# Two-layer encoder trunk on one core: MLP products with both activation parts in 512 moving columns, and the norm chains placed first

## The chip, the cores and the metric

The kernel runs on one core of one Trainium2 chip. The metric is the device time of one execution in microseconds. A core has TensorE (PE) for matrix products, VectorE (DVE), ScalarE (ACT) and GpSimd (POOL) for work on tiles in SBUF, and DMA queues, here nearly all issued by SyncE (SP). PE adds its products up in PSUM, and DVE or ACT fetches them from there.

## The reference

Two layers run over 256 tokens of 2048 channels, in float32. Each layer has a modulated RMSNorm, a mixer with three kinds of heads behind one input projection, an output projection, a second modulated RMSNorm and an MLP with a squared ReLU and 8192 hidden channels. The six modulation vectors of a layer come from one condition vector and a matrix of 2048 x 12288.

```python
cond = jax.nn.silu(c)
for layer in range(DEPTH):                                   # 2
    mod = (cond @ ada_w[layer] + ada_b[layer])[:, None, :]
    sh_a, sc_a, g_a, sh_m, sc_m, g_m = jnp.split(mod, N_MOD, axis=-1)
    h = rmsnorm(x, norm_mix_w[layer]) * (1.0 + sc_a) + sh_a
    x = x + g_a * hybrid_mixer(h, ..., w_in[layer], ..., w_out[layer])
    h = rmsnorm(x, norm_mlp_w[layer]) * (1.0 + sc_m) + sh_m
    x = x + g_m * (jnp.square(jax.nn.relu(h @ w_ff1[layer])) @ w_ff2[layer])
return rmsnorm(x, final_norm_w)
```

## The kernel before

**Products.** Activations lie with channels on the partitions and the 256 tokens beside each other. Every large product is made of two parts per operand: ACT casts a weight tile to `wh` (L221), and DVE or POOL subtracts that from the tile and gives the rest, `wl` (L227; `pool_share` says what part goes to POOL). The activations have a high and a low part too (`hh`, `hl` for the normalised input). `mm_b` (L252 to L254) then does three matmuls of 256 columns for each 128x128 weight tile, with `wh` and the low part, `wl` and the high part, `wh` and the high part, into one of four quarters of a PSUM tile of 1024 columns (`pair`, named pj in the profile, of which there are two in turn). `mm_a` (L263 to L265) is the form of the mixer with 512 columns of weights moving.

**Stages.** Layer 0 has its input projection in groups of contraction tiles, with the modulation vectors coming in beside it; then the mixer heads, the output projection (four blocks `nb` of 512 columns, `residual` at L796 adds each to X), and the MLP. Weights come as chunks of 512 KB (`raw`, six buffers), 508 of them for the MLP. `ff1` makes a block of 512 hidden channels, `square` applies Relu (L964), Square (L969), a cast (L971) and a subtraction (L972) and so gives the block's two parts, `ff2` takes eight contraction tiles of two such blocks through four blocks of 512 output columns and adds them to X with four updates (L796) for each PSUM tile. `ff2_tail` does the last quarter of the last layer in narrower pieces.

**Norm chains.** Behind the last residual of a stage the sum of squares must be ready before the next stage can run. `stat_piece` squares a quarter of X and adds (L372 to L375), `stat_sum` adds over the partitions on PE (L383), a Newton iteration gives the inverse root (L393, L351 to L357), `stat_spread` sends it to all partitions (L401, then R by ACT at L405), and `h_make` forms the normalised input (L492 to L500). To keep PE at work meanwhile, `lead` computes the first block of the next projection from X that is not normalised yet (operand made at L432 to L437, products of 258 columns at L471 to L473) and `lead_out` corrects it afterwards (L485).

**Modulation vectors.** A tile of `ada_w` (512 KB, 380 of them) is multiplied by the condition on DVE (L283), with a running sum. `rate`, `step` and `pump` hand out how many of these tiles are issued in which stage; a DMA for them is issued behind the weight DMA nine back (WIN = 8).

**Order.** The Tile framework sets each engine's instruction order from the program order, priorities and simulated readiness; each engine then works through its list in that order. An instruction whose input is late holds up everything behind it on its engine.

## Time and profile before

| | us |
|---|---|
| median of 3 runs | 2548.88 |
| lowest and highest | 2541.46, 2551.96 |
| the profiled execution | 2549.75 |
| its span in the trace | 2548.0 |
| PE, DVE, ACT, POOL busy | 2450.1, 1583.2, 1180.9, 758.9 |

The mean granted clock of PE is 0.977 of 2.4 GHz. A row of a timeline begins with start and duration in us. The duration of a matmul contains its way through the array, and consecutive ones overlap, so what a matmul costs in a row is read from one start to the next. In groups by line, "x" is the count, and behind the bar stand busy us, mean ns of one, and idle us ahead with what ended it.

### The profile page before, as it was taken

Reading aid. Unit: us, or ns where it says so; the run is one execution under the profiler, and the core shown is the slowest. Engines: PE = TensorE matmul, PEld = TensorE weight load, DVE = VectorE, ACT = ScalarE, POOL = GpSimd, SP = SyncE. Lnnn points to the kernel's source line nnn. Section 1 sums busy time; section 2 is a strip of 40 time slices with the busy share of each in tenths; the row PEclk is TensorE's granted clock in tenths of the full one; section 3 lists DMA queues with packets and bytes.
Section 4 is the critical chain, followed back from the end, with each engine's and each line's share of the span. In section 5 each row is a group of like instructions: output and inputs, shape, how many; then the busy total and the mean of one; then the engine's idle time right before and its main releaser. Section 6 shows DMA issues by size and latency. Waiting matters only on the chain.

```text
span 2548.0 us, 46455 instructions
## 1 busy us (share of the span) xinstructions
PE 2450.1 (96%) x19016; PEld 2378.3 (93%) x19016; DVE 1583.2 (62%) x2427; ACT 1180.9 (46%) x1442; POOL 758.9 (30%) x314
## 2 busy tenths in 40 slices
PE   7999998979999999999989999999999999999997
PEld 6899977979999999999988989899999999999997
DVE  5867878788655444444478777656754555555554
ACT  4444455535544444444446446454644444344443
POOL 4786531212676766767650000000000000000000
PEclk8999999989999999999989999999999999999998
DMA  9899867788998888888867777555555555555552
GB/s 359 299 327 329 305 217 265 285 299 338 322 334 310 279 288 297 287 280 298 285 213 241 272 247 266 192 166 178 178 182 186 188 182 183 187 185 183 186 187 91
DMA packets 177246, 630.45 MB, mean 247 GB/s; under 512 B 19588, under 2 KB 24326, under 8 KB 177032
## 3 DMA queue, kind: packets, MB, share of 16 engines
q1 hardware_dynamic: 176600, 627.08, 70.8%
q8 instruction: 149, 2.44, 0.4%
q14 instruction: 65, 0.53, 0.1%
q10 hardware_dynamic: 432, 0.39, 0.1%
HBM read 625.30 MB, written 2.10 MB: 246 GB/s over the span
## 4 chain that ended last, share of the span: by engine, by line
PE 79%; DVE 9%; DMA 4%; issue 3%; POOL 3%; ACT 2%; SPq 0%; DVEq 0%; POOLq 0%; ACTq 0%
PE pj L253 23%; PE pj L252 23%; PE pj L254 23%; DMA ada<-ada_w 3%; POOL wl L227 3%; DVE ada L283 2%; PE pj L264 2%; PE pj L265 2%; PE pj L263 2%; DVE wl L227 2%; PE mx L620 1%; ACT wh L221 1%; DVE cv L709 1%; DVE blk L437 0%; DMA raw<-ada_w 0%
## 5 line engine op out<-in xcount | busy, mean ns | idle before, releaser
L221 ACT CAST wh<-raw 128x1024 fp32r<-128x1024 f32 x804 | 840.4, 1047 | 1129.8 <-PE pj L254 881.3
L227 POOL TENSOR_TENSOR wl<-raw,wh 128x1024 fp32r<-128x1024 f32 (+1 forms) x309 | 756.3, 2451 | 583.4 <-ACT wh L221 565.3
L227 DVE TENSOR_TENSOR wl<-raw,wh 128x1024 fp32r<-128x1024 f32 x495 | 615.7, 1246 | 487.4 <-ACT wh L221 486.7
L252 PE MATMUL pj<-hl,wh 128*128 128x256 f32 x2912 | 830.9, 286 | 9.5 <-DVE hl L500 8.2
L253 PE MATMUL pj<-hh,wl 128*128 128x256 f32 x2912 | 830.4, 285 | 7.2 <-DVE wl L227 7.2
L254 PE MATMUL pj<-hh,wh 128*128 128x256 f32 x2912 | 828.1, 284 | 0.0
L253 PE MATMUL pj<-blk,wl 128*128 128x256 f32 x2528 | 713.6, 282 | 6.6 <-DVE wl L227 5.2
L252 PE MATMUL pj<-blk,wh 128*128 128x256 f32 x2528 | 712.8, 282 | 2.8 <-ACT blk L538 1.5
L254 PE MATMUL pj<-blk,wh 128*128 128x256 f32 x2528 | 711.3, 281 | 0.0
L283 DVE SCALAR_TENSOR_TENSOR ada<-ada,cond 128x1024 f32<-128x1024 f32 x380 | 456.7, 1214 | 227.7 <-DMA ada<-ada_w 225.6
L252 PEld LDWEIGHTS pj<-hl,wh 128*128 128x128 f32 x2912 | 561.8, 193 | 10.7 <-DVE hl L500 8.9
L253 PEld LDWEIGHTS pj<-hh,wl 128*128 128x128 f32 x2912 | 562.4, 193 | 9.3 <-DVE wl L227 8.7
L254 PEld LDWEIGHTS pj<-hh,wh 128*128 128x128 f32 x2912 | 562.1, 193 | 0.2
L253 PEld LDWEIGHTS pj<-blk,wl 128*128 128x128 f32 x2528 | 478.5, 189 | 7.3 <-DVE wl L227 5.6
L252 PEld LDWEIGHTS pj<-blk,wh 128*128 128x128 f32 x2528 | 478.8, 190 | 3.4 <-ACT blk L538 1.9
L254 PEld LDWEIGHTS pj<-blk,wh 128*128 128x128 f32 x2528 | 479.3, 190 | 0.0
L1045 POOL TENSOR_TENSOR blk<-blk,R 128x1024 f32<-128x1024 f32 x1 | 2.4, 2357 | 1199.1 <-ACT R L405 1199.1
L264 PE MATMUL pj<-wl,hh 128*128 128x512 f32 x384 | 155.4, 405 | 8.5 <-DVE wl L227 8.4
L796 DVE SCALAR_TENSOR_TENSOR X<-pj,mod,X 128x256 f32<-128x256 f32 x284 | 117.8, 477 | 64.0 <-PE pj L254 63.9
L263 PE MATMUL pj<-wh,hl 128*128 128x512 f32 x384 | 153.2, 399 | 1.2 <-ACT wh L221 1.2
L265 PE MATMUL pj<-wh,hh 128*128 128x512 f32 x384 | 152.9, 398 | 0.0
L264 PEld LDWEIGHTS pj<-wl,hh 128*128 128x128 f32 x384 | 73.7, 192 | 24.5 <-DVE wl L227 10.7
(232 smaller groups left out, 1648.0 us busy)
## 6 DMA issues: line engine op xcount, KB each, us to landing
raw<-w_ff SPq DMA_DIRECT2D x508, 512.0 KB, 4.1
ada<-ada_w SPq DMA_DIRECT2D x380, 512.0 KB, 6.3
raw<-w_in SPq DMA_DIRECT2D x224, 512.0 KB, 5.0
raw<-w_out SPq DMA_DIRECT2D x64, 512.0 KB, 4.4
X<-x SPq DMA_DIRECT2D x4, 512.0 KB, 6.2
...
```

Of the source, the lines that this page charges most:

```text
L221: nc.scalar.copy(hi, raw)
L227: eng.tensor_tensor(lo, raw, hi.bitcast(F32), ALU.subtract)
L252: nc.tensor.matmul(o, lhsT=wh[:, s], rhs=al, start=st, stop=False, skip_group_check=True)
L253: nc.tensor.matmul(o, lhsT=wl[:, s], rhs=ah, start=False, stop=False, skip_group_check=True)
L254: nc.tensor.matmul(o, lhsT=wh[:, s], rhs=ah, start=False, stop=last, skip_group_check=True)
L263: nc.tensor.matmul(o, lhsT=al[:, s], rhs=wh, start=first, stop=False)
L264: nc.tensor.matmul(o, lhsT=ah[:, s], rhs=wl, start=False, stop=False)
L265: nc.tensor.matmul(o, lhsT=ah[:, s], rhs=wh, start=False, stop=last)
L283: nc.vector.scalar_tensor_tensor(raw, raw, 1.0, self.cond, ALU.mult, ALU.mult, accum_out=self.part[l][:, i, h:h + 1])
L620: nc.tensor.matmul(ps[:, i * P:i * P + P], lhsT=lt, rhs=v[:, j, c:c + P], start=first, stop=last, skip_group_check=True)
L709: V.scalar_tensor_tensor(y[:, s:], x[:, n, :T - s], w[:, 3 - s:4 - s], y[:, s:], ALU.mult, ALU.add)
L796: V.scalar_tensor_tensor(self.X(k), ps[:, n * T:n * T + T], self.mod[l][:, c:c + 1], self.X(k), ALU.mult, ALU.add)
```

## The change

Two parts. In the MLP, the two parts of the activations lie beside each other in one tile (`h`, and the tiles that `square` returns), and `mm_w` does one matmul of `wh` with the 512 columns of both parts and one of `wl` with the 256 of the high part. A PSUM tile of 1024 columns now holds two output tiles instead of four, each as two halves that must be added; so `ff1` fetches with a copy (or an addition) and an addition, each 512 wide, and `ff2` runs eight blocks of 256 columns and updates X with twice as many instructions. Weight chunks of the MLP are four contraction tiles by 256 columns, the same bytes and count. Relu and Square become one DVE instruction. The second part puts the instructions of the norm chains under a higher priority, issues no modulation tile in the last block of the output projection, in the leading block or in the last `ff2` of a layer, and takes POOL off the subtractions there. `stat_sum`, `stat_spread`, `early`, `lead_out` and `h_make` are wrapped as `stat_piece` is. The core of the diff:

```diff
-            pool_win=[...], pool_late=0.5, pool_out=0.3, pool_ff1=[0.3, 0.8], pool_ff=0.8),
+            pool_win=[...], pool_late=0.5, pool_out=0.3, pool_ff1=[0.0, 0.8], pool_ff=0.8),
...
+URGENT = 400
...
+    def chunk2(self, src):
+        raw = self.raw.tile([P, 4, 256], F32, tag="raw", name=self.name("raw"))
+        self.wdma.append(self.nc.sync.dma_start(raw, src))
+        hi, lo = self.split(raw, 4, 256)
+        return [(hi[:, i, :], lo[:, i, :]) for i in range(4)]
+
+    def mm_w(self, ps, w, act, first, last):
+        nc = self.nc
+        wh, wl = w
+        for n in range(2):
+            s = slice(n * P, n * P + P)
+            o = ps[:, n * 512:n * 512 + 512]
+            nc.tensor.matmul(o.rearrange("p (a b) -> p a b", b=T), lhsT=wh[:, s], rhs=act, start=first, stop=False,
+                             skip_group_check=True)
+            nc.tensor.matmul(o[:, :T], lhsT=wl[:, s], rhs=act[:, 0, :], start=False, stop=last, skip_group_check=True)
+
+    def sums(ps):
+        v = ps.rearrange("p (n c) -> p n c", c=512)
+        return v[:, :, 0:T], v[:, :, T:2 * T]
...
-    def flush(self):
-        while self.fixes:
+    def flush(self, age=2):
+        for f in self.fixes:
+            f[3] += 1
+        while self.fixes and self.fixes[0][3] >= age:
...
     def stat_piece(self, q):
+        with self.tc.high_priority(offset=URGENT):
+            self.stat_piece_(q)
...
@@ lead
-            w = self.chunk(wsrc(k0, nk), nk)
-            if js == 3:
-                self.step(nk / 4)
+            w = wsrc(k0, nk)
@@ output projection
-        self.rate(cfg["ada_out"], 16)
+        self.rate(cfg["ada_out"], 12)
...
-                self.step()
+                if nb != 3:
+                    self.step()
             if kcs[-1] == 3:
-                self.residual(l, 2, nb, pairs.pop(nb))
+                with self.tc.high_priority(offset=URGENT * (nb == 3)):
+                    self.residual(l, 2, nb, pairs.pop(nb))
@@ ff1
+        for h in range(2):
+            ps = self.pair()
+            for k0 in range(kts[0], kts[-1] + 1, 4):
+                w = self.chunk2(self.io["w_ff1"][l, 2 * b + h, k0 // 4])
+                for k in range(k0, k0 + 4):
+                    self.mm_w(ps, w[k - k0], self.h[:, k], k == kts[0], k == kts[-1])
+                self.step(0.5)
+            d = t[:, 2 * h:2 * h + 2, :]
+            p0, p1 = self.sums(ps)
+            if fresh:
+                nc.scalar.copy(d, p1)
+            else:
+                nc.vector.tensor_tensor(d, p1, d, ALU.add)
+            nc.vector.tensor_tensor(d, p0, d, ALU.add)
@@ square
+        nc.vector.scalar_tensor_tensor(t, t, 0.0, t, ALU.max, ALU.mult)
+        for h in range(2):
+            s = self.slot((P, 2, 2, T), F32R)
+            nc.scalar.copy(s[:, 0], t[:, 2 * h:2 * h + 2, :])
+            nc.vector.tensor_tensor(s[:, 1], t[:, 2 * h:2 * h + 2, :], s[:, 0].bitcast(F32), ALU.subtract)
@@ ff2
         if last:
             self.stat_begin()
+            self.pool_share = 0.0
+            self.per = 0.0
-        for nb in range(3 if tail else 4):
+        for nb in range(6 if tail else 8):
...
+                    self.mm_w(ps, w[i], hid[c](i), c == 0 and i == 0, c == 1 and i == 3)
+                self.step(0.5)
+            for n in range(2):
+                k = 2 * nb + n
+                g = self.mod[l][:, 5 * KT + k:5 * KT + k + 1]
+                with self.tc.high_priority(offset=URGENT * last):
+                    for c in range(n * 512, n * 512 + 512, T):
+                        V.scalar_tensor_tensor(self.X(k), ps[:, c:c + T], g, self.X(k), ALU.mult, ALU.add)
```

On PE in the MLP, two weight tiles of the first `ff1` block behind the leading one stand like this before (hl and hh are the two parts of the input, the numbers those of buffers):

```order
L252 MATMUL pj811_5676<-hl_96,wh816_5685 128x256
L253 MATMUL pj811_5676<-hh_95,wl817_5686 128x256
L254 MATMUL pj811_5676<-hh_95,wh816_5685 128x256
L252 MATMUL pj811_5676<-hl_96,wh816_5685 128x256
L253 MATMUL pj811_5676<-hh_95,wl817_5686 128x256
L254 MATMUL pj811_5676<-hh_95,wh816_5685 128x256
```

and in the changed kernel (h holds both parts):

```order
L259 MATMUL pj808_5664<-h_95,wh810_5667 128x512
L261 MATMUL pj808_5664<-h_95,wl811_5668 128x256
L259 MATMUL pj808_5664<-h_95,wh810_5667 128x512
L261 MATMUL pj808_5664<-h_95,wl811_5668 128x256
```

Six matmuls of 256 columns became two of 512 and two of 256.

On DVE in `ff2` of layer 0, updates of X and modulation tiles stand in this order before (L283 is a modulation tile, L796 an update, L227 a weight subtraction):

```order
L796 SCALAR_TENSOR_TENSOR X0_91<-pj1040_7288,mod0_126,X0_91 128x256 x4
L283 SCALAR_TENSOR_TENSOR ada1054_7412,part1_125<-ada1054_7412,cond_109 128x1024
L283 SCALAR_TENSOR_TENSOR ada1068_7540,part1_125<-ada1068_7540,cond_109 128x1024
L227 TENSOR_TENSOR wl1076_7560<-raw1074_7557,wh1075_7559 128x1024
L283 SCALAR_TENSOR_TENSOR ada1069_7543,part1_125<-ada1069_7543,cond_109 128x1024
L796 SCALAR_TENSOR_TENSOR X1_92<-pj1055_7419,mod0_126,X1_92 128x256 x4
L283 SCALAR_TENSOR_TENSOR ada1083_7671,part1_125<-ada1083_7671,cond_109 128x1024
L283 SCALAR_TENSOR_TENSOR ada1084_7674,part1_125<-ada1084_7674,cond_109 128x1024
L283 SCALAR_TENSOR_TENSOR ada1092_7742,part1_125<-ada1092_7742,cond_109 128x1024
L796 SCALAR_TENSOR_TENSOR X2_93<-pj1070_7550,mod0_126,X2_93 128x256 x4
L227 TENSOR_TENSOR wl1096_7751<-raw1094_7748,wh1095_7750 128x1024
```

and in the changed kernel, where L308 is the modulation tile and L1055 the update:

```order
L1055 SCALAR_TENSOR_TENSOR X0_91<-pj1051_6985,mod0_125,X0_91 128x256
L308 SCALAR_TENSOR_TENSOR ada1065_7079,part1_124<-ada1065_7079,cond_108 128x1024
L1055 SCALAR_TENSOR_TENSOR X0_91<-pj1051_6985,mod0_125,X0_91 128x256 x3
L308 SCALAR_TENSOR_TENSOR ada1066_7082,part1_124<-ada1066_7082,cond_108 128x1024
L1055 SCALAR_TENSOR_TENSOR X0_91<-pj1058_7034,mod0_125,X0_91 128x256 x4
L308 SCALAR_TENSOR_TENSOR ada1078_7161,part1_124<-ada1078_7161,cond_108 128x1024
L1055 SCALAR_TENSOR_TENSOR X1_92<-pj1067_7089,mod0_125,X1_92 128x256 x3
L227 TENSOR_TENSOR wl1086_7197<-raw1084_7194,wh1085_7196 128x1024
L1055 SCALAR_TENSOR_TENSOR X1_92<-pj1067_7089,mod0_125,X1_92 128x256
L308 SCALAR_TENSOR_TENSOR ada1079_7164,part1_124<-ada1079_7164,cond_108 128x1024
L308 SCALAR_TENSOR_TENSOR ada1094_7265,part1_124<-ada1094_7265,cond_108 128x1024
L1055 SCALAR_TENSOR_TENSOR X1_92<-pj1074_7138,mod0_125,X1_92 128x256 x4
```

A PSUM tile's four updates came once in two or three modulation tiles, and now come once in one or two, at times with a tile or a subtraction between them.

On PE at the end of the leading block of layer 1, before (L471 to L473 are leading products, L401 is the spread of the inverse root, on which R rests):

```order
L472 MATMUL mx1873_14217<-blk1869_14201,wl1898_14426 128x258
L473 MATMUL mx1873_14217<-blk1869_14201,wh1897_14425 128x258
L471 MATMUL mx1874_14218<-blk1869_14201,wh1897_14425 128x258
L401 MATMUL pj1872_14216<-ident_113,nw1883_14286 128x128 x2
L472 MATMUL mx1874_14218<-blk1869_14201,wl1898_14426 128x258
L473 MATMUL mx1874_14218<-blk1869_14201,wh1897_14425 128x258
L471 MATMUL pj1871_14215<-blk1869_14201,wh1897_14425 128x258
L472 MATMUL pj1871_14215<-blk1869_14201,wl1898_14426 128x258
```

and in the changed kernel, where L513 to L515 are the leading products, L440 is the spread and L579 the first of the gate products, which read the normalised input:

```order
L514 MATMUL pj1914_12438<-blk1913_12431,wl1944_12655 128x258
L515 MATMUL pj1914_12438<-blk1913_12431,wh1943_12654 128x258
L513 MATMUL pj1914_12438<-blk1913_12431,wh1943_12654 128x258
L514 MATMUL pj1914_12438<-blk1913_12431,wl1944_12655 128x258
L515 MATMUL pj1914_12438<-blk1913_12431,wh1943_12654 128x258
L440 MATMUL pj1915_12439<-ident_112,nw1926_12509 128x128 x2
L579 MATMUL mx1954_12768<-h_95,wh1956_12771 76x256
L580 MATMUL mx1954_12768<-h_95,wl1957_12772 76x256
```

The spread stood 32 leading products ahead of their end, and now stands behind the last.

## Rows read from the trace of the kernel before

**Rows 1.** Page, busy time of each engine, share of span, instructions:

```profile
PE 2450.1 (96%) x19016; PEld 2378.3 (93%) x19016; DVE 1583.2 (62%) x2427; ACT 1180.9 (46%) x1442; POOL 758.9 (30%) x314
```

**Rows 2.** Page, the chain that ended last, by engine:

```profile
PE 79%; DVE 9%; DMA 4%; issue 3%; POOL 3%; ACT 2%; SPq 0%; DVEq 0%; POOLq 0%; ACTq 0%
```

**Rows 3.** Stretches: us; PE, PEld, DVE, ACT, POOL busy; PEclk; DMA share; GB/s:

```profile
350.00:500.00 150.00, 133.20 (x844) 118.86 (x844) 113.23 (x243) 74.15 (x117) 33.55 (x14) 0.92 0.71 256
500.00:610.00 110.00, 94.03 (x718) 92.65 (x718) 97.97 (x159) 51.20 (x77) 19.45 (x8) 0.91 0.86 311
610.00:1290.00 680.00, 680.00 (x5708) 680.00 (x5707) 341.28 (x504) 298.94 (x294) 457.71 (x186) 1.00 0.86 301
1290.00:1350.00 60.00, 48.08 (x343) 46.87 (x342) 43.88 (x91) 30.69 (x54) 24.63 (x11) 0.86 0.53 181
...
1850.00:2510.00 660.00, 660.00 (x5548) 660.00 (x5548) 348.03 (x368) 286.20 (x284) 0.00 (x0) 1.00 0.55 183
```

**Rows 4.** Stretch inside layer 1's MLP, PE alone: us, busy (x), clock, DMA:

```profile
1900.00:2400.00 500.00, 500.00 (x4201) 1.00 0.55 185
```

**Rows 5.** Timeline of PE where a run of 512 columns ends:

```profile
1396.63 0.39 PE L265 MATMUL pj<-wh,hh 128*128 128x512 f32 x1
...
1398.67 0.39 PE L265 MATMUL pj<-wh,hh 128*128 128x512 f32 x1
...
1399.01 0.28 PE L253 MATMUL pj<-hh,wl 128*128 128x256 f32 x1
```

**Rows 6.** Timeline of PE at a lone 512 between 256s:

```profile
243.00 0.40 PE L263 MATMUL pj<-wh,hl 128*128 128x512 f32 x1
243.24 0.28 PE L253 MATMUL pj<-hh,wl 128*128 128x256 f32 x1
243.35 0.28 PE L254 MATMUL pj<-hh,wh 128*128 128x256 f32 x1
```

**Rows 7.** Groups by line of DVE and ACT in 1850 to 2510:

```profile
L227 DVE TENSOR_TENSOR wl<-raw,wh 128x1024 fp32r<-128x1024 f32 x231 | 282.8, 1224 | 295.9 <-ACT wh L221 295.8
...
L972 DVE TENSOR_TENSOR blk<-blk,blk 128x1024 fp32r<-128x1024 f32 x14 | 17.1, 1218 | 0.0
...
L964 ACT ACTIVATE blk<-pj 128x1024 f32<-128x1024 f32 x14 | 14.4, 1026 | 25.7 <-PE pj L254 25.7
```

**Rows 8.** Waits and groups of DVE in 610 to 1290, then its timeline:

```profile
DVE ada L283 <- DMA ada<-ada_w: 173.5, 47, 8.9
...
DVE X L796 <- PE pj L254: 36.9, 15, 6.1
...
L796 DVE SCALAR_TENSOR_TENSOR X<-pj,mod,X 128x256 f32<-128x256 f32 x120 | 49.7, 477 | 36.9 <-PE pj L254 36.9
...
867.68 1.22 DVE L283 SCALAR_TENSOR_TENSOR ada<-ada,cond 128x1024 f32<-128x1024 f32 x1 [8.52 <-DMA ada<-ada_w]
...
868.82 1.66 DVE L796 SCALAR_TENSOR_TENSOR X<-pj,mod,X 128x256 f32<-128x256 f32 x4
```

**Rows 9.** Timeline of DVE, and one row of PE, at layer 0's end:

```profile
1295.85 4.44 DVE L437 SCALAR_TENSOR_TENSOR blk<-X,mod,blk 128x256 fp32r<-128x256 f32 x11
...
1307.12 1.66 DVE L796 SCALAR_TENSOR_TENSOR X<-pj,mod,X 128x256 f32<-128x256 f32 x4 [3.53 <-PE pj L254]
...
1313.44 2.00 DVE L374 TENSOR_TENSOR ss<-ss,blk 128x512 f32<-128x512 f32 x1
1315.36 5.48 DVE L437 SCALAR_TENSOR_TENSOR blk<-X,mod,blk 128x256 fp32r<-128x256 f32 x3
1320.77 1.21 DVE L283 SCALAR_TENSOR_TENSOR ada<-ada,cond 128x1024 f32<-128x1024 f32 x1
...
1322.31 0.68 DVE L375 TENSOR_TENSOR ss<-ss,blk 128x512 f32<-128x512 f32 x1
...
1323.04 1.87 PE L383 MATMUL pj<-ones,ss 128*128 128x1 f32 x8 [6.12 <-DVE ss L375]
...
1337.27 1.29 DVE L492 TENSOR_TENSOR ht<-X,R 128x512 f32<-128x512 f32 x2 [5.37 <-ACT R L405]
```

More of the change, by code (lines that the diff above doesn't have):

```diff
@@ L478, in lead, with lead_win, get, lead_ff1 @@
         return ps
+    def lead_win(self, l):
+        def get(k, nk):
+            w = self.chunk(self.io["w_in"][l, 0, k // 4][:, k % 4:k % 4 + nk, :], nk)
+            return lambda i, n: tuple(x[:, n * P:n * P + P] for x in w[i])
+        return get
+    def lead_ff1(self, l):
+        def get(k, nk):
+            w = [self.chunk2(self.io["w_ff1"][l, b, k // 4]) for b in range(2)]
+            return lambda i, n: tuple(x[:, n % 2 * P:n % 2 * P + P] for x in w[n // 2][i])
+        return get
     def lead_out(self, ps, dst, func=AF.Identity, scale=1.0):
+        with self.tc.high_priority(offset=URGENT):
+            self.lead_out_(ps, dst, func, scale)
+    def lead_out_(self, ps, dst, func, scale):
         nc = self.nc
@@ L957, in ff1 @@
-        if acc is not None:
-            t = acc
-            d = self.flat(t)
-            nc.vector.tensor_tensor(d, ps, d, ALU.add)
-            nc.scalar.activation(t, t, AF.Relu)
-        else:
-            t = self.slot()
-            nc.scalar.activation(self.flat(t), ps, AF.Relu)
-        return self.square(t)
+        done = kts[-1] == KT - 1
+        fresh = acc is None
+        t = self.slot() if fresh else acc
+        for h in range(2):
[9 more added lines that the diff above has]
+                nc.scalar.copy(d, p1)
+            else:
+                nc.vector.tensor_tensor(d, p1, d, ALU.add)
+            nc.vector.tensor_tensor(d, p0, d, ALU.add)
@@ L967, in square @@
+        return self.square(t) if done else t
     def square(self, t):
         nc = self.nc
-        nc.scalar.activation(t, t, AF.Square)
-        hi, lo = self.slot(dt=F32R), self.slot(dt=F32R)
-        nc.scalar.copy(hi, t)
-        nc.vector.tensor_tensor(lo, t, hi.bitcast(F32), ALU.subtract)
-        return hi, lo
+        nc.vector.scalar_tensor_tensor(t, t, 0.0, t, ALU.max, ALU.mult)
+        out = []
+        for h in range(2):
+            s = self.slot((P, 2, 2, T), F32R)
+            nc.scalar.copy(s[:, 0], t[:, 2 * h:2 * h + 2, :])
+            nc.vector.tensor_tensor(s[:, 1], t[:, 2 * h:2 * h + 2, :], s[:, 0].bitcast(F32), ALU.subtract)
+            out.append(s)
@@ L975, in ff2 @@
+        return lambda i: out[i // 2][:, :, i % 2, :]
     def ff2(self, l, s, hid, last):
+        V = self.nc.vector
         if last:
             self.stat_begin()
+            self.pool_share = 0.0
+            self.per = 0.0
         tail = last and l == DEPTH - 1
-        for nb in range(3 if tail else 4):
+        for nb in range(6 if tail else 8):
+            if last and nb >= 6:
+                self.early(CFG[l + 1]["early_win"], nb - 6, l + 1, 0, 1)
             ps = self.pair()
             for c in range(2):
-                if nb == 3 and last:
-                    self.early(CFG[l + 1]["early_win"], c, l + 1, 0, 1)
-                w = self.chunk(self.io["w_ff2"][l, nb, 2 * s + c], 4)
-                hi, lo = hid[c]
+                w = self.chunk2(self.io["w_ff2"][l, nb, 2 * s + c])
@@ L993, in ff2 @@
+            if last and nb % 2 == 1:
+                self.stat_piece(nb // 2)
+                if nb == 7:
                     self.early(CFG[l + 1]["early_win"], 2, l + 1, 0, 1)
             if tail:
-                for n in range(4):
-                    self.final_scale(4 * nb + n)
+                for n in range(2):
+                    self.final_scale(2 * nb + n)
         if tail:
```

97 lines of the change are left out of this document (44 added, 53 removed).

## The prediction

> **What bounds the kernel now.** I read the page first, then the stretches, then the starts of single matmuls. TensorE is busy 96% of the span [rows 1], and the chain that ended last lies 79% on it, with 9% on VectorE and 4% on DMA [rows 2]. The table of stretches says where the rest is lost [rows 3]. In the two MLP stretches, 610 to 1290 (layer 0) and 1850 to 2510 (layer 1), PE is busy for all of 680 and 660 us at granted clock 1.00 (2.4 GHz). There only fewer or cheaper matmuls can shorten anything. The lost time sits at the seams: 500 to 610 (PE busy 94.03 of 110 us, clock 0.91), from the out-projection of layer 0 to its MLP, and 1290 to 1350 (48.08 of 60, clock 0.86), from layer 0 to layer 1. So the change has two separate prices: the matmuls of the MLP, and the norm chains at the seams.
>
> **The MLP products.** The order of the changed kernel has 14816 matmuls of PE instead of 18784: 3968 fewer. Each of 3968 products (one 128x128 weight tile) goes from three matmuls of 256 columns to one of 512 and one of 256. The columns stay 768, so all that can be saved is what a matmul costs beyond its columns.
>
> The old price: 4201 matmuls of 256 in 500.00 us, 119.0 ns each, so 357.0 ns for a product [rows 4]. For 512 columns there are the older products of the mixer: from the start at 1396.63 to that at 1398.67 nine matmuls, 2.04 / 9 = 227 ns each [rows 5]. Twice 119.0 would be 238, so a matmul joined saves 11 ns. The alternation 512, 256, 512, 256 does not occur before, so I bound it:
> - Where a run of 512 ends, the last 512 and the first 256 take 1398.67 to 1399.01, 0.34 us [rows 5]. That is the low end, 340.5 ns, a gain of 16.5 per product.
> - One lone 512 stands between 256s: it and the next 256 take 243.00 to 243.35, 0.35 us [rows 6]. That is the high end, about 351, a gain of 6.
> - In steady streams the two prices add up: 227 + 119 = 346, a gain of 11.
>
> I take 346: it lies between the ends and is the sum of two long averages, while each end is one junction. 3968 x 11 ns = **43.6 us**; the ends are 65.5 and 23.8 us. The 227 and the 119 are at granted clock 1.00, as the MLP stretches are.
>
> The Trainium skill (TensorE: Matmul & The Clock Gate, Back-to-back issue gap) speaks against this: spacing is columns / 2.4 GHz plus about 2.5 ns. By it 256 would cost 109.2 and 512 215.8 ns (my estimates), a product 327.5 before and 325.0 after, and the gain would be 3968 x 2.5 ns = 9.9 us. The rows do not agree: 119.0 and 227.
>
> **What pays for it on the other engines.** In layer 1 nothing shows. VectorE gets, per layer, some 126 more residual updates at 0.41 us (four take 1.66 [rows 8]; 52 us), 32 additions of 512 elements at about 0.69, as L375 alone takes [rows 9] (22 us), and 16 squarings of 1024 at about 1.22, as L972 takes [rows 7] (20 us), some 94 us in all. Layer 1 has VectorE at 348 of 660 us [rows 3], and its weight subtractions wait 296 us for ScalarE [rows 7]. ScalarE loses the Relu (1.03 us [rows 7]) and the Square of each block, of the same size, and gets two copies of half the width. I cost this at nothing; the cover is some 300 us of VectorE idle per layer.
>
> Layer 0 has less cover in time, not in sum. VectorE works there 341 of 680 us, but 173.5 us of its waiting is for the modulation tiles' DMA (47 waits, the longest 8.9), and behind such a wait stand the residual updates, which set PSUM free [rows 8]. At 867.68 a tile had been waited for 8.52 us, and the four updates came directly behind it [rows 8]. Only 15 of the 30 groups of four updates waited for PE at all (36.9 us) [rows 8]; the others found their products long done. A pair buffer may now be late by the length of the next pair: before 32 products x 0.357 = 11.4 us, after 16 x 0.346 = 5.5. In the new order about 13 of layer 0's 64 pairs of ff2 have two or more modulation tiles between them and the update before. One tile costs 1.14 us (starts 868.82 less 867.68) [rows 8], so 13 x 0 to 1.14 = 0 to 15 us; I take **+5**, as GpSimd's subtractions and the blocks of ff1 move slack about. The weight stream must run about 3% faster where DMA is at 0.86 over the stretch [rows 3] and higher at its beginning: **+3** (0 to 6).
>
> **The norm chains.** From layer 0 to 1 (1290 to 1350) the chain is: last residual at 1307.12, squares, sum at L374, the leading products' operand at L437, L375, then PE's sum at 1323.04 after 6.12 us idle; later VectorE waits 5.37 us for R at 1337.27 [rows 9]. From 1307.12 to the end of L375 at 1322.99 pass 15.9 us. L374 took 2.00 us and three L437 5.48, with GpSimd at work beside them; alone eleven L437 took 4.44, 0.40 each [rows 9]. One tile of 1.14 stands between L437 and L375. With GpSimd off and the chain first, residual 1.66, two sums of 0.69, four L437 of 0.4 and a square of about 1.03 (as L964 [rows 7]) are 5.7 us: up to 10 us less, and some 3 of the 0.14 x 60 = 8 us that the clock costs there [rows 3]. Against it: in the new order PE's spread (L440) stands behind all leading products and directly ahead of the gate products, where before 32 matmuls lay behind it; what hid R's 5.4 us is now ahead of it. Two to three us return. I take **-8** (-13 to 0).
>
> In layer 0's own seam (500 to 610) the tiles that before stood beside the chain go into the out-projection ahead of it (19 over 12 steps instead of 16). VectorE is busy 97.97 of 110 us there [rows 3], so work that only moves is not gained. **-2** (-8 to +6), and **+2** for 350 to 500, where the 19 tiles come earlier and VectorE is busy 113 of 150 us. At the end the last sums stand behind one more weight subtraction of 1.22 [rows 7] and the added updates: **+2** (0 to 3).
>
> **Sum.** -43.6 + 5 + 3 - 8 - 2 + 2 + 2 = -41.6 us. The profiled execution took 2549.75 us (span 2548.0), 0.9 over the median of 2548.88; 2549.75 - 41.6 = **2508 us**. A measurement of this kernel can tell about 0.5% from no change: faster is below 2536, slower above 2562.
>
> **Rivals.**
> - The alternation runs at the low end of 340.5 ns, because a 256 behind a 512 keeps costing 114. For it: every run of 512 ends so. Against: the lone 512 was dearer. 2508 - 21.9 = 2486 us; chance 0.10.
> - It runs at the high end, 351: each 512 behind a 256 stays dear. 2508 + 19.8 = 2528 us; chance 0.08.
> - The cost goes by columns, with nothing saved by joining: a 512 in the alternation takes 2 x 119.0. Then -43.6 falls out and 2552 us are left, no change that can be told. Against it: 227 over nine starts. Chance 0.06. The skill's rule above is nearly this one, with 2542 us.
> - The seams gain nothing: spread behind the leading products costs what GpSimd and tiles gave back. For it: VectorE's load in the seam hardly falls. 2508 + 10, and up to 8 more if layer 0's seam loses: 2518 to 2526 us; chance 0.11.
> - Slower: in layer 0's ff2 the residual updates come late behind tiles that wait for DMA. It decides where the updates of a pair end over 5.5 us after its products; the wait of 8.9 exceeds that. 64 pairs late by 1.2 us cost 77 us instead of 5: 2580 us; from 0.92 us each on it is slower than 2562. Against it: the mean wait is 173.5 / 47 = 3.7 us, and half of the updates already wait for PE. Chance 0.07, of which 0.02 stays within 0.5%.
>
> **How the numbers follow.** My forecast holds 0.58 with its own spread of 2495 to 2522. Faster by over 0.5%: 0.58 + 0.10 + 0.08 + 0.11 = 0.87; within: 0.06 + 0.02 = 0.08; slower: 0.05. The range leaves out the costs by columns, the late updates and the best of the low end: 2484 to 2540.
>
> **What would show it.** In the profile after, a stretch of layer 1's MLP must show two matmuls per 346 ns and PE busy all through at clock 1.00; 340 or 351 tells the ends apart. Layer 1's MLP should shorten by some 21 us, layer 0's by 15 to 20. PE waiting on a residual update of VectorE in layer 0 would be the late updates; more than 1 us per pair makes me wrong. At the seam to layer 1, L374 to L375 should take under 4 us instead of 9.6, and PE's wait ahead of its sum fall below 3 us. If instead PE waits longer behind the leading products, the seam has only moved its gap.

## The result and the profile after

| | before | after |
|---|---|---|
| median, us | 2548.07 (6 runs) | 2564.47 (6 runs) |
| lowest and highest | 2541.46, 2551.96 | 2560.53, 2573.67 |
| profiled execution | 2549.75 | 2573.67 |
| ratio after / before | | 1.007, 95% interval 1.0052 to 1.0088 |

The changed kernel is 0.7% slower, outside the range of 2484 to 2540. Its profiled execution was the slowest of the six, 9.2 us over the median, so single microseconds of its trace are read below beside the other kernels' traces. First the page's busy times and the table of stretches, to set beside [rows 1, 3] (columns as there):

```profile
PE 2436.4 (95%) x15048; PEld 2179.1 (85%) x15048; DVE 1822.5 (71%) x2849; ACT 1154.8 (45%) x1468; POOL 692.9 (27%) x286
...
610.00:1290.00 680.00, 662.32 (x3743) 575.53 (x3742) 459.45 (x677) 274.36 (x294) 429.01 (x173) 0.99 0.81 289
1290.00:1350.00 60.00, 52.05 (x320) 47.81 (x319) 52.18 (x102) 26.20 (x36) 0.00 (x0) 0.89 0.65 223
1350.00:1700.00 350.00, 323.19 (x2178) 297.13 (x2177) 261.22 (x461) 178.30 (x268) 0.00 (x0) 0.97 0.71 243
```

PE has 3968 matmuls less and is busy only 13.7 us less. Layer 0's MLP, which had PE busy for all of 680 us, now has it idle for 17.7 us, and VectorE there went from 341 to 459 us.

Where the time went is seen in the stages, cut at events that each trace has: the first residual update of layer 0's output projection, the first leading product of its MLP, the last update of its `ff2`, the spread of layer 1's first norm, the first residual update of layer 1's output projection, the last leading product of its MLP, and its last `ff2` update ahead of the tail. Times in us, from the profiled executions; the names of the experiments come below.

| kernel | to out 0 | out 0 | lead and MLP 0 | seam | mixer 1 | out 1, lead | MLP 1 | tail |
|---|---|---|---|---|---|---|---|---|
| before | 478 | 66 | 765 | 27 | 395 | 82 | 701 | 33 |
| after | 486 | 61 | 782 | 26 | 408 | 82 | 693 | 34 |
| e1, wide products alone | 477 | 66 | 789 | 29 | 395 | 82 | 691 | 34 |
| e2, second part alone | 482 | 68 | 771 | 24 | 402 | 82 | 700 | 33 |
| e3, wide in layer 1 alone | 480 | 64 | 771 | 28 | 396 | 82 | 690 | 34 |
| e5, after, squares' subtractions on GpSimd | 481 | 65 | 767 | 25 | 404 | 82 | 692 | 33 |
| e6, after, matmuls grouped | 480 | 63 | 776 | 23 | 404 | 82 | 690 | 34 |
| e8, e3 grouped | 478 | 66 | 772 | 28 | 393 | 82 | 690 | 34 |
| e10, after, tiles as before | 478 | 65 | 784 | 27 | 397 | 82 | 690 | 34 |
| e11, e3 with GpSimd in MLP 1 | 478 | 64 | 773 | 27 | 395 | 82 | 696 | 31 |
| e12, e1 with a lighter VectorE | 481 | 65 | 767 | 19 | 395 | 82 | 692 | 34 |
| e13, e3 with priorities | 479 | 65 | 768 | 23 | 394 | 82 | 689 | 34 |
| e14, e12, priorities, GpSimd off at the seam | 476 | 65 | 774 | 24 | 398 | 82 | 693 | 34 |
| e15, e12 with priorities | 484 | 65 | 761 | 19 | 395 | 82 | 691 | 34 |
| e16, after, GpSimd kept at the seam | 484 | 61 | 793 | 18 | 406 | 82 | 692 | 34 |

In the changed kernel layer 0 up to the end of its MLP loses some 20 us, the mixer of layer 1 13 (7 to 11 in the other kernels that keep the tiles out of the seams), and only layer 1's MLP gains: 8 us (8 to 12 in the other kernels with wide products there, but for e11) of some 21 that I had said would go.

**The products.** The stretch of layer 1's MLP that answers to [rows 4], and starts of matmuls within it that answer to [rows 5, 6]:

```profile
1900.00:2400.00 500.00, 500.00 (x2852) 1.00 0.56 188
```

```profile
1999.86 0.40 PE L259 MATMUL pj<-h,wh 128*128 128x512 f32 x1
2000.09 0.28 PE L261 MATMUL pj<-h,wl 128*128 128x256 f32 x1
2000.20 0.40 PE L259 MATMUL pj<-h,wh 128*128 128x512 f32 x1
2000.44 0.28 PE L261 MATMUL pj<-h,wl 128*128 128x256 f32 x1
2000.56 0.40 PE L259 MATMUL pj<-h,wh 128*128 128x512 f32 x1
```

2852 matmuls are 1426 products, so 350.6 ns each, where 357 stood before; in the other kernels' traces it is 349 to 351. The 512s take 0.23 and 0.24 us, not 0.227.

**Layer 0's MLP.** What PE waited for in 575 to 1330 (us in total, times, longest), and VectorE's list ahead of one of these waits with the PE row that it ends:

```profile
PE pj L259 <- DVE X L1055: 15.4, 6, 5.4
PE pj L259 <- DVE blk L1019: 5.9, 5, 1.6
```

```profile
854.44 4.59 DVE L1030 TENSOR_TENSOR blk<-blk,blk 128x512 fp32r<-128x512 f32 x2
858.96 1.21 DVE L308 SCALAR_TENSOR_TENSOR ada<-ada,cond 128x1024 f32<-128x1024 f32 x1
...
860.09 1.91 DVE L1055 SCALAR_TENSOR_TENSOR X<-pj,mod,X 128x256 f32<-128x256 f32 x4
...
862.15 0.47 PE L259 MATMUL pj<-blk,wh 128*128 128x512 f32 x1 [2.14 <-DVE X L1055]
```

L1030 is the squares' subtraction of 512 elements. Two of them held VectorE for 4.5 us, a modulation tile for 1.1 more, and the four updates that set a PSUM tile free stood behind. VectorE had not stopped since 850.32: it was busy, not behind a DMA. So it is for nine of the eleven waits on updates and additions, 17 of their 21 us: in the 14 us ahead of each VectorE did not wait for a DMA. Ahead of the other two it had waited for a modulation tile, by 7.14 us (at 1035.02, ahead of a PE wait of 1.86 at 1048.36) and by 1.72 (at 1228.93, ahead of 2.58 at 1238.19). In sum VectorE's waits for the tiles' DMA in 610 to 1290 fell to half of the 173.5 us of [rows 8]:

```profile
DVE ada L308 <- DMA ada<-ada_w: 87.1, 45, 7.6
```

The groups of VectorE in layer 0 (610 to 1290), then in layer 1 (1850 to 2510), and at the end the squares' subtraction of 1024 elements in layer 0 before (610 to 1290):

```profile
L1030 DVE TENSOR_TENSOR blk<-blk,blk 128x512 fp32r<-128x512 f32 x32 | 51.8, 1648 | 3.4 <-ACT blk L1029 3.4
L1025 DVE SCALAR_TENSOR_TENSOR blk<-blk 128x1024 f32<-128x1024 f32 x16 | 32.9, 2054 | 0.4
L1019 DVE TENSOR_TENSOR blk<-pj,blk 128x512 f32<-128x512 f32 x39 | 26.8, 686 | 30.5 <-ACT blk L1016 30.3
...
L227 DVE TENSOR_TENSOR wl<-raw,wh 128x1024 fp32r<-128x1024 f32 x60 | 78.9, 1315 | 45.3 <-ACT wh L221 45.3
...
L227 DVE TENSOR_TENSOR wl<-raw,wh 128x1024 fp32r<-128x1024 f32 x234 | 286.0, 1222 | 186.5 <-ACT wh L221 186.4
...
L1030 DVE TENSOR_TENSOR blk<-blk,blk 128x512 fp32r<-128x512 f32 x32 | 21.2, 684 | 0.0
...
L1025 DVE SCALAR_TENSOR_TENSOR blk<-blk 128x1024 f32<-128x1024 f32 x16 | 19.6, 1225 | 0.5
...
L972 DVE TENSOR_TENSOR blk<-blk,blk 128x1024 fp32r<-128x1024 f32 x16 | 36.5, 2284 | 29.3 <-ACT blk L971 29.3
```

With GpSimd at work beside it (layer 0) L1030 takes 1648 ns, without (layer 1) 684; the squaring (L1025) 2054 and 1225; the weight subtractions that are left to VectorE (L227) 1315 and 1222; the additions from PSUM (L1019) take 686 in layer 0 too. The Trainium skill (SBUF — State Buffer, Who interferes with whom) says that a VectorE instruction with two inputs in SBUF contends with a GpSimd instruction that reads SBUF; these rows agree, in that only the instructions without a PSUM input are slowed, L227 though by 8% alone.

**The mixer of layer 1.** VectorE's list and the PE row that ends the wait, first before, then after:

```profile
1646.28 1.22 DVE L682 TENSOR_TENSOR blk<-blk,blk 128x1024 f32<-128x1024 f32 x1
1647.41 2.35 DVE L227 TENSOR_TENSOR wl<-raw,wh 128x1024 fp32r<-128x1024 f32 x2
...
1648.69 0.80 PE L264 MATMUL pj<-wl,hh 128*128 128x512 f32 x1 [3.23 <-DVE wl L227]
...
1674.26 1.22 DVE L308 SCALAR_TENSOR_TENSOR ada<-ada,cond 128x1024 f32<-128x1024 f32 x1 [1.77 <-DMA ada<-ada_w]
...
1677.68 1.21 DVE L308 SCALAR_TENSOR_TENSOR ada<-ada,cond 128x1024 f32<-128x1024 f32 x1
...
1679.96 2.35 DVE L227 TENSOR_TENSOR wl<-raw,wh 128x1024 fp32r<-128x1024 f32 x2
...
1681.23 0.80 PE L289 MATMUL pj<-wl,h 128*128 128x512 f32 x1 [7.38 <-DVE wl L227]
```

L680 to L682, now L743 to L745, are the rotary chain, five instructions. Before, they ran from 1641.73 on with nothing between them; now two modulation tiles stand inside the chain, the subtraction behind it is late, and PE waits 7.38 us where before it waited 3.23 at the same place. Counted in the traces, 62 modulation tiles run in this stage after, 52 before; ahead of layer 0's output projection 135 instead of 128; in its lead and MLP 169 instead of 179. Every kernel here with 62 tiles in this mixer has 6.9 to 7.7 us at that place, every one with 52 has 3.2, and only those with 62 have a wait of 2.2 us for ScalarE some 100 us earlier.

**The seam to layer 1.** PE's rows that answer to that at 1323.04 in [rows 9], at the end of layer 0's MLP and behind it:

```profile
1312.52 0.77 PE L259 MATMUL pj<-blk,wh 128*128 128x512 f32 x1 [5.37 <-DVE X L1055]
...
1339.06 1.02 PE L414 MATMUL pj<-ones,ss 128*128 128x1 f32 x8 [1.41 <-DVE ss L406]
...
1361.57 0.50 PE L579 MATMUL mx<-h,wh 128*76 128x256 f32 x1 [5.77 <-DVE h L563]
```

The wait ahead of the sum fell from 6.12 to 1.41 us, as forecast; 5.77 us stand ahead of the gate products instead, which now wait for the first normalised input, and 5.37 ahead of the last pair of `ff2`. From the start of L405 to the end of L406 (L374 and L375 before) 4.0 us pass instead of 9.6, where I had said under 4. Between the last update and the spread six modulation tiles run, as many as before, and ahead of one of them VectorE still waits 2.54 us for its DMA.

### The profile page after: what moved, and what is told of

Same layout as the page of the kernel before. It is cut to its first block, busy times and chain, and to the rows that moved or that the text cites. A ratio compares the mean times of both kernels' runs of the same rounds, so it can differ in the third digit from the quotient of the medians.

```text
span 2571.9 us, 38934 instructions
## 1 busy us (share of the span) xinstructions
PE 2436.4 (95%) x15048; PEld 2179.1 (85%) x15048; DVE 1822.5 (71%) x2849; ACT 1154.8 (45%) x1468; POOL 692.9 (27%) x286
## 4 chain that ended last, share of the span: by engine, by line
PE 75%; DVE 12%; DMA 6%; issue 3%; ACT 2%; POOL 1%; SPq 0%; DVEq 0%; ACTq 0%; POOLq 0%
PE pj L259 32%; PE pj L261 16%; PE pj L278 5%; PE pj L277 5%; DMA ada<-ada_w 5%; PE pj L279 5%; DVE ada L308 3%; DVE wl L227 3%; PE pj L289 2%; PE pj L290 2%; PE pj L288 2%; DVE blk L1030 1%; ACT wh L221 1%; POOL wl L227 1%; PE mx L683 1%
## 5 line engine op out<-in xcount | busy, mean ns | idle before, releaser
L227 DVE TENSOR_TENSOR wl<-raw,wh 128x1024 fp32r<-128x1024 f32 x523 | 650.4, 1245 | 342.1 <-ACT wh L221 341.5
L227 POOL TENSOR_TENSOR wl<-raw,wh 128x1024 fp32r<-128x1024 f32 (+1 forms) x281 | 690.3, 2460 | 578.0 <-ACT wh L221 558.5
L259 PE MATMUL pj<-blk,wh 128*128 128x512 f32 x2016 | 714.3, 397 | 16.7 <-DVE X L1055 15.4
L259 PE MATMUL pj<-h,wh 128*128 128x512 f32 x1952 | 689.8, 398 | 7.9 <-DVE blk L1019 4.8
L261 PE MATMUL pj<-blk,wl 128*128 128x256 f32 x2016 | 568.7, 282 | 0.0
L308 DVE SCALAR_TENSOR_TENSOR ada<-ada,cond 128x1024 f32<-128x1024 f32 x380 | 458.2, 1213 | 144.7 <-DMA ada<-ada_w 143.5
L261 PE MATMUL pj<-h,wl 128*128 128x256 f32 x1952 | 548.7, 281 | 2.2 <-DVE wl L227 1.5
L259 PEld LDWEIGHTS pj<-blk,wh 128*128 128x128 f32 x2016 | 381.6, 189 | 108.9 <-issue 12.2
L259 PEld LDWEIGHTS pj<-h,wh 128*128 128x128 f32 x1952 | 367.2, 188 | 97.9 <-DVE h L563 4.0
L261 PEld LDWEIGHTS pj<-h,wl 128*128 128x128 f32 x1952 | 369.6, 189 | 3.2 <-DVE wl L227 2.1
L1055 DVE SCALAR_TENSOR_TENSOR X<-pj,mod,X 128x256 f32<-128x256 f32 x504 | 231.3, 480 | 83.8 <-PE pj L261 78.4
L277 PE MATMUL pj<-h,wh 128*128 128x256 f32 x960 | 277.8, 290 | 10.1 <-DVE h L563 6.8
L278 PE MATMUL pj<-h,wl 128*128 128x256 f32 x960 | 278.5, 290 | 4.3 <-DVE wl L227 4.3
L279 PE MATMUL pj<-h,wh 128*128 128x256 f32 x960 | 275.7, 287 | 0.0
L277 PEld LDWEIGHTS pj<-h,wh 128*128 128x128 f32 x960 | 187.6, 196 | 11.2 <-DVE h L563 6.9
L278 PEld LDWEIGHTS pj<-h,wl 128*128 128x128 f32 x960 | 188.1, 196 | 6.1 <-DVE wl L227 5.5
L279 PEld LDWEIGHTS pj<-h,wh 128*128 128x128 f32 x960 | 187.8, 196 | 0.2
L289 PE MATMUL pj<-wl,h 128*128 128x512 f32 x384 | 154.8, 403 | 15.9 <-DVE wl L227 15.0
L288 PE MATMUL pj<-wh,h 128*128 128x512 f32 x384 | 153.3, 400 | 1.7 <-ACT wh L221 1.7
```

The costliest lines, as they stand in the source:

```text
L227: eng.tensor_tensor(lo, raw, hi.bitcast(F32), ALU.subtract)
L259: nc.tensor.matmul(o.rearrange("p (a b) -> p a b", b=T), lhsT=wh[:, s], rhs=act, start=first, stop=False, skip_group_check=True)
L261: nc.tensor.matmul(o[:, :T], lhsT=wl[:, s], rhs=act[:, 0, :], start=False, stop=last, skip_group_check=True)
L277: nc.tensor.matmul(o, lhsT=wh[:, s], rhs=al, start=st, stop=False, skip_group_check=True)
L278: nc.tensor.matmul(o, lhsT=wl[:, s], rhs=ah, start=False, stop=False, skip_group_check=True)
L279: nc.tensor.matmul(o, lhsT=wh[:, s], rhs=ah, start=False, stop=last, skip_group_check=True)
```

## Experiments

Each kernel's ratio is to the kernel before, in interleaved runs on the same chip.

**e1, the first part alone, and e2, the second alone.** e1 is the changed kernel with

```diff
-URGENT = 400
+URGENT = 0
-        self.rate(cfg["ada_out"], 12)
+        self.rate(cfg["ada_out"], 16)
-                if nb != 3:
-                    self.step()
+                self.step()
-            self.pool_share = 0.0
-            self.per = 0.0
```

and with the rates of the leading block, `flush` and `pool_ff1` as before (`flush` hands out `mod_fix`, which makes a modulation vector of finished tiles; the change delays it); e2 is the kernel before with the opposite edits and the `high_priority` blocks.

> The first part alone: products with 512 columns in both layers, priorities off, modulation tiles, GpSimd share and the emission of mod_fix as before. Theory (the changed kernel is eaten from two sides: late PSUM updates in layer 0's MLP, and modulation tiles moved into the mixers): PE saves 6.4 ns x 3968 = 25 us, the late updates in 610 to 1290 cost about 20, so 2540 to 2550. Rival (the whole loss comes from the second part): 2520 to 2526, no PE waits on L1055 or L1019 in layer 0.

> The second part alone: three matmuls of 256 columns as before, with the priorities, the modulation tiles kept out of the seams, delayed mod_fix and GpSimd off at the seams. Theory: the tiles kept out of the seams land in the mixers and hold a rotary or weight chain there, about +12 in layer 1's and +5 in layer 0's mixer, and the seams give back less than that: 2553 to 2565. Rival (my forecast): the seams gain 8 to 10, 2538 to 2542.

e1: median 2565.41 us, ratio 1.0071 (1.0056 to 1.0086). e2: 2561.56 us, 1.0054 (1.0038 to 1.0069). Each half alone is slower than before, and the two together are no slower than one. e1 was worse than my 2540 to 2550: all its loss is lead and MLP 0, 789 us instead of 765. There I had costed the late updates at about 20, and they and the clock (granted 0.98 in 575 to 1310, before 1.00) were nearer 37 (24 lost, and 13 of PE's gain eaten). e2 came out as the theory had it: mixer 402 instead of 395, the way to the output projection 482 instead of 478, the seam 24 instead of 27; that lead and MLP 0 took 6 us more was not in it. Why the losses do not add is not settled. That the tiles which e2's edits take out of layer 0's MLP relieve the stage that e1 overloads was my guess; but with 161 tiles behind the leading block lead and MLP 0 took 776, 782 and 793 us (e6, after, e16), and with 173 it took 784 and 789 (e10, e1).

**e3, 512 columns in layer 1 alone**; layer 0 keeps its methods and weight layout.

```diff
+        if l == 0:
+            return self.ff1_n(l, b, kts, acc)
...
+        if l == 0:
+            return self.ff2_n(l, s, hid, last)
```

> The 512-column products in layer 1's MLP alone, all else as before. Theory: layer 1 has no GpSimd and no modulation tiles in its MLP, so the 1984 products keep 6.4 ns each: -12.7 us, 2533 to 2538. Rival (late updates come with the smaller PSUM tiles wherever they are): 2545 to 2555.

Median 2543.8, ratio 0.9992 (0.998 to 1.0003), profiled 2547.17. MLP 1 took 690 us instead of 701, near the 12.7 us of 1984 x 6.4 ns, and nothing waits there for an update. In the total 3 of these 11 us arrive, between the ranges of the theory and of the rival. In this trace the instructions of layer 0's MLP stand in the order of before, yet the stage has two PE waits of 1.8 us on a subtraction (at 861 and 1266) and, behind the second, a granted clock of 0.66 in 1265 to 1270; in e8, which is the same there, one such wait followed a modulation tile that came after 8.50 us where before it came after 6.82. So layer 0's MLP was at an edge already; what moved the DMA by these microseconds was not tried.

**e4, matmuls alone.** Streams of 192 products on resident tiles; the rest of the computation is left out.

> Streams of matmuls on resident weights and activations, nothing else of the computation: 192 products each of (1) three 256 columns, (2) 512 and 256 in turn, (3) 512, 512, 256, 256, (4) eight 512 and eight 256, (5) as 2 with the two parts 512 elements apart, (6) as 2 with one weight tile for both, (7) 512 alone. Theory, the alternation itself costs: 357, 351, 346, 343, 351 ns for a product, 351 for (6), 227 for one matmul of (7). Rival, something else of the kernel (SBUF traffic of DVE and ACT) makes the 351: (2) is 346 or less and (3), (4) are the same as (2). Second rival, the strided operand costs: (5) is over (2).

The first rows of the streams in PE's timeline (narrow, its end, grouped by two, grouped by eight, strided, one weight tile):

```profile
81.18 0.28 PE L46 MATMUL pj<-h,wh 128*128 128x256 f32 x1
...
150.18 0.52 PE L46 MATMUL pj<-h,wh 128*128 128x256 f32 x2
...
218.14 0.40 PE L46 MATMUL pj<-h,wh 128*128 128x512 f32 x1
...
285.02 0.40 PE L46 MATMUL pj<-h,wh 128*128 128x512 f32 x1
...
352.06 0.40 PE L46 MATMUL pj<-g,wh 128*128 128x512 f32 x1
...
419.90 0.40 PE L46 MATMUL pj<-h,wh 128*128 128x512 f32 x1
```

The narrow stream is 575 matmuls from 81.18 to 150.18, 120.0 ns each, 360 a product. The alternation begins one matmul later, at 150.30, and lasts until 218.14: 67.84 / 192 = 353 ns. Grouped 512, 512, 256, 256 it is 66.88 / 192 = 348, eight and eight 349, where I had expected 343, with the parts apart 353 and with one weight tile for both 353. So the alternation has its own price, with no other engine at work; neither the strided operand nor the second weight tile makes it (that a weight load goes with each matmul, here too, was not varied). In the stream of 512 columns alone a matmul takes 227 ns; between two of 256 columns it takes 236.

**e6, the changed kernel grouped, and e8, e3 grouped.**

```diff
         for n in range(2):
             nc.tensor.matmul(..., lhsT=wh[:, s], rhs=act, ...)
+        for n in range(2):
             nc.tensor.matmul(..., lhsT=wl[:, s], rhs=act[:, 0, :], ...)
```

> The changed kernel, with the two 512-column products of a contraction tile first and then the two of 256 columns. In the stream of matmuls alone that order cost 348.7 ns a product instead of 353.0. Theory (the price of the junctions holds in the kernel): 4.3 x 1984 = -8.5 us in layer 1's MLP, and up to as much in layer 0's unless the late updates take it: 2548 to 2558. Rival (in the kernel other traffic sets the pitch): no change, 2562 to 2568.

> 512-column products in layer 1's MLP alone, grouped as 512, 512, 256, 256; the rest as before. Theory: layer 1's MLP gains (7.0 + 4.3) x 1984 = 22 us over before, so 2546.8 - 22 = 2525; with what the ungrouped kernel of this kind did not show of its gain (3 us in the median instead of 12), 2525 to 2536. Rival (the gain of layer 1 is given back somewhere behind): 2540 to 2546.

e6: 2555.69, ratio 1.003 (1.0018 to 1.0042). e8: 2542.71, 0.9974 (0.9963 to 0.9985). The junction theory fell in the kernel: 1900 to 2400 of e8 and of e3 hold 2859 and 2867 matmuls, 349.8 and 348.8 ns a product, so grouping gave nothing there. e6's median lies in the theory's range, 9 us under that of after, but not by the theory: of the 20 us between the profiled executions MLP 1 has 3 and layer 0's MLP 6, and the rest is scattered over stages whose code is the same. It is left open.

**e5, the squares' subtractions of layer 0 on GpSimd.**

```diff
-            nc.vector.tensor_tensor(s[:, 1], ...)
+            eng = nc.gpsimd if self.pool_share > 0 else nc.vector
+            eng.tensor_tensor(s[:, 1], ...)
```

> The changed kernel, with the subtractions of the squared blocks (L1030) on GpSimd in layer 0 instead of VectorE, where two of them took up to 5.0 us beside GpSimd and stood ahead of residual updates. Theory (updates come late because VectorE is busy with subtractions that GpSimd slows): the PE waits on L1055 in layer 0's MLP fall by half or more and that stage by 8 to 12 us, 2550 to 2558. Rival (updates late behind modulation tiles that wait for DMA): the stage keeps its length, 2562 to 2568.

2552.43 us, ratio 1.001 (0.9997 to 1.0022). Lead and MLP 0 fell from 782 to 767, and PE's waits there from 15.4 on updates and 5.9 on additions to 8.5 and 1.3 (575 to 1330, us in total, times, longest):

```profile
PE pj L259 <- DVE X L1056: 8.5, 4, 6.0
PE pj L261 <- POOL wl L227: 5.0, 8, 1.7
...
PE pj L259 <- DVE blk L1019: 1.3, 1, 1.3
```

The theory holds: behind the leading block the modulation tiles are the same in number (161), and 12 us of the 16 lost came back by taking 52 us of slowed subtractions from VectorE; 5.0 us of waits for GpSimd are the price.

**e11, GpSimd in layer 1's MLP**, e3 with `pool_ff=0.8` and `pool_ff1=[0.8]` in layer 1.

> 512-column products in layer 1's MLP alone, now with GpSimd doing four fifths of the weight subtractions there, as in layer 0; no modulation tiles run there. Theory A (GpSimd's slowing of the squares' subtractions makes updates late by itself): two of these subtractions take 4 us or more as in layer 0, and PE waits for updates by 5 us or more in all, the stage from update to update at 695 us or more instead of 690. Theory B (it takes the modulation tiles in the list as well): the subtractions are slow, but PE does not wait, 688 to 692 us.

2544.82, ratio 0.9986 (0.9975 to 0.9998). In layer 1, 1890 to 2490:

```profile
PE pj L259 <- ACT wh L221: 1.0, 1, 1.0
PE pj L259 <- DVE X L1117: 1.0, 1, 1.0
...
L1092 DVE TENSOR_TENSOR blk<-blk,blk 128x512 fp32r<-128x512 f32 x26 | 49.7, 1943 | 7.6 <-ACT blk L1091 7.6
```

The subtractions are slowed to 1943 ns, more than in layer 0, and PE waits 2 us. So the slowing alone makes no late updates. VectorE was busy 266 of 640 us here, and 459 of 680 in layer 0 of the changed kernel, where the modulation tiles run: that is theory B, though the stage, 696 us by the table, lies in theory A's range; the tail is 3 us shorter, and of the other 3 the waits explain two. A busy VectorE alone makes no late updates either. In layer 1 of the changed kernel it is nearly as busy as in layer 0, without GpSimd and without tiles, and PE waits for no update there (1850 to 2510, columns as in [rows 3]):

```profile
1850.00:2510.00 660.00, 658.12 (x3743) 572.76 (x3742) 440.49 (x550) 285.52 (x313) 0.00 (x0) 1.00 0.56 187
```

Layer 0 has all three, a busy VectorE, slowed instructions and tiles in the list; which two of them would do was not tried.

**e10, the changed kernel with tiles, `mod_fix` and GpSimd as before**, priorities on.

> The changed kernel with the priorities, but with modulation tiles, mod_fix and GpSimd's share at the seams as before. Theory (the tiles that left the seams cost 12 us in layer 1's mixer and 4 in front, and relieve layer 0's MLP by 8 to 10): mixer of layer 1 back at 395 to 398 us, layer 0's MLP at 770, so 2560 to 2568 in all. Rival (the priorities themselves hold up the mixers): the mixer of layer 1 stays at 405 or more.

2561.91, ratio 1.0045 (1.0029 to 1.0061). Mixer 1 took 397 us and lead and MLP 0 784 (768 without the leading block), both as the theory had it. This kernel differs from e1 in the priorities alone and is no slower. Over all traces with 62 tiles in that mixer (after, e2, e5, e6, e16) it takes 402 to 408 us, over all with 52 393 to 398. So it is not the priorities that cost the mixer some 9 us, but the tiles that moved: the rows above show them in the rotary chain. The later `mod_fix` is in the same five kernels and was not tried by itself; GpSimd's share differs among the five.

**e12, VectorE lighter**: e1, with e5's edit and

```diff
-        nc.vector.scalar_tensor_tensor(t, t, 0.0, t, ALU.max, ALU.mult)
+        nc.scalar.activation(t, t, AF.Relu)
+        nc.scalar.activation(t, t, AF.Square)
```

> 512-column products in both layers, no priorities, tiles as before; in layer 0 the squares' subtractions on GpSimd and Relu and Square on ScalarE in both layers, so that VectorE has 85 us less to do in layer 0's MLP. Theory (VectorE's load there makes the late updates): layer 0's MLP from 773 to 740 to 750 us, in all 2534 to 2545. Rival (the smaller PSUM tiles lose their time to tiles that wait for DMA): layer 0's MLP stays over 758 and the total at 2550 or more.

2533.31, ratio 0.9936 (0.9915 to 0.9957): faster than before. PE's waits on updates and additions (575 to 1330) and VectorE's waits for the tiles' DMA (610 to 1290), first e1, then e12:

```profile
PE pj L259 <- DVE X L1054: 16.7, 8, 5.3
PE pj L259 <- DVE blk L1020: 7.4, 4, 4.7
PE pj L515 <- DVE X L1054: 5.2, 1, 5.2
...
DVE ada L308 <- DMA ada<-ada_w: 104.6, 48, 6.7
...
PE pj L259 <- DVE X L1056: 7.6, 5, 3.3
PE pj L259 <- DVE blk L1020: 5.0, 2, 4.7
...
DVE ada L308 <- DMA ada<-ada_w: 132.2, 68, 6.7
```

With a lighter VectorE PE waited less than half as long, 12.6 us instead of 29.3, although VectorE waited longer for the tiles. So their DMA is not what makes most of the updates late. Lead and MLP 0 went from 789 to 767, and the seam from 29 to 19, which I had not foreseen: its chain runs on VectorE too. The stage of the MLP without the leading block was 752, a little over my 740 to 750; VectorE still has 390 of 680 us there.

**e13, e3 with the priorities and GpSimd off at the seam**, tiles as before.

> 512-column products in layer 1's MLP alone, with the priorities and with GpSimd off at layer 0's end and in its leading block, but with the modulation tiles and mod_fix where they were. Theory (what the seam gives comes from GpSimd and priority, what the mixers lose from moved tiles): from the last update of layer 0 to the spread 24 us instead of 27.4, the mixer of layer 1 at 395 to 398, in all 2538 to 2543. Rival (the seam gains only when the tiles leave it): 27 us there, 2543 to 2548.

2534.47, ratio 0.9947 (0.9929 to 0.9964), better than the theory's 2538. The seam is 23 us, mixer 1 394.

**e14, both together; e15, e14 with GpSimd kept; e16, the changed kernel with GpSimd kept.**

What e14 has over e15:

```diff
-            ..., pool_ff1=[0.3, 0.8], pool_ff=0.8),
+            ..., pool_ff1=[0.0, 0.8], pool_ff=0.8),
...
+            self.pool_share = 0.0
```

> The changed kernel with the priorities and with GpSimd off at layer 0's end, but with the modulation tiles and mod_fix where they were before, Relu and Square on ScalarE, and layer 0's squares' subtractions on GpSimd. Theory: the two gains add where they do not touch the same seam; layer 0's MLP at 748 to 752, layer 1's mixer at 394 to 397, layer 1's MLP at 690 to 693, from layer 0's last update to the spread 19 to 24 us: 2522 to 2533 in all. Rival (both took their gain at the same seam, and without GpSimd the last updates of layer 0 come late): 2533 to 2540.

> The lighter VectorE kernel (512-column products in both layers, Relu and Square on ScalarE, layer 0's squares' subtractions on GpSimd, tiles as before) with the priorities on and GpSimd kept at layer 0's end. Theory (GpSimd off made VectorE late for the last updates of layer 0, 6.0 us at 1298 instead of 2.9, and the stage longer): back to 2530 to 2536. Rival (the priorities did it, since spread then stands behind the leading products and PE waits 5.8 us for the first normalised input): 2540 to 2548.

> The changed kernel with GpSimd kept in layer 0's last ff2 and in its leading block; all else as changed. Theory: the wait ahead of the last pair of layer 0 (5.4 us on L1055) shrinks to about 3, the slowed DVE work beside GpSimd gives 1 to 3 of it back, 2558 to 2564. Rival: the wait stays, as the order and not VectorE's load sets it: 2564 to 2570.

e14: 2546.95, ratio 0.9996 (0.9986 to 1.0005). e15: 2527.71, 0.9923 (0.991 to 0.9936), the lowest median here. e16: 2570.87, 1.0083 (1.0067 to 1.0099). e14 is slower than both of its ranges, e15 faster than both, e16 just slower than both. Between e14 and e15 lies only GpSimd's share in the last `ff2` and the first group of layer 0's MLP, and 19 us. What PE waited for at the seam, first e14 (1290 to 1350), then e15 (1280 to 1360):

```profile
PE pj L259 <- DVE X L1057: 6.0, 1, 6.0
PE mx L581 <- DVE h L565: 5.8, 1, 5.8
...
PE pj L259 <- DVE X L1056: 4.0, 1, 4.0
PE mx L581 <- DVE h L565: 2.7, 3, 1.3
```

With wide products GpSimd off puts all subtractions on VectorE, in front of the last updates, and the wait for the normalised input grows. But that GpSimd kept makes the whole faster held in the lighter kernel alone. In e16 the seam did shrink, from 26 to 18 us, and lead and MLP 0 grew by 11, with 17.3 us of PE waits on updates between 570 and 1280 instead of 10.0; the sum was no better. Why the share at the end moves the stage before it is open: the counter behind `pool_share` runs on, so that other subtractions fall to GpSimd and the scheduler's order changes with them.

## Why the prediction was wrong

- **What bounds the kernel** held: MLP 1 is PE alone and gained by matmuls alone, at clock 1.00.
- **The price of a product** was mis-sized. I took 346 ns, the sum of two steady streams, over the bound of 351 that a single junction gave [rows 6]. The runs show 350.6, and 353 in the stream alone. The gain is 3968 x 6.4 = 25 us instead of 43.6: 18 us of the miss. The rival at the high end, to which I gave 0.08, had this term right. I held one lone 512 for a chance reading; it was the only row that had the alternation in it. The steady average of 227 does not hold between 256s.
- **Layer 0's cover** was the step that failed worst. I costed the squarings once, by layer 1's rows (1.22 us), put the squares' subtractions, of which two of 512 replace one of 1024, at nothing more, and wrote that in layer 0 the cover was short "in time, not in sum". There a squaring takes 2.05 us, and the two subtractions 3.30 where one took 2.28; the additions cost 0.69 as I had counted. The old trace had said so already: in 610 to 1290 L972 took 2284 ns a piece beside GpSimd, against the 1218 of [rows 7], and I did not carry it into the sum. VectorE got 118 us more there, not 94; in layer 1 it got 92. Of the late updates I had the place, but the wrong cause (tiles that wait for DMA): nine of eleven waits have no such wait ahead of them, and in e12 PE's waits fell while VectorE's waits for the tiles grew. e5, e11 and e12 show what it was instead, a VectorE list that is too long for the smaller PSUM tile, with slowed subtractions in it. The +5 became some +30, 21 us of it waits and some 7 PE's clock (granted 0.99 in 575 to 1310, before 1.00). That rival, as I wrote it, came half true: late updates, at some 30 us instead of its 77, by 6 waits on updates instead of 64, and my sign for it, over 1 us per pair, stood at 0.24.
- **The tiles that leave the seams** were not costed where they go. I followed them into the out-projection, +2, and not into the mixers: some +9 in layer 1 (e10) and 3 to 4 ahead of layer 0's output projection, where the ranges overlap (128 tiles: 476 to 484 us, 135: 480 to 486).
- **The seam** had the right mechanism against it and too large a gain: -8 became -1 to -4. The sum's wait fell as predicted, and the gap moved to the gate products, as the rival said. I had counted GpSimd off the subtractions as part of the gain; in the two pairs that differ in GpSimd's share alone the seam is shorter with GpSimd kept, 19 us against 24 (e15, e14) and 18 against 26 (e16, after).
- Together: -25 by products, +30 in layer 0 (both signs estimated from the waits above and the stages), +12 by tiles, -3 at the seam make +14, against 16 measured; the terms are read from single profiled executions, so the agreement is no proof of each.
